# Delta rule of a hybrid decoder: one chain of small operations for two chunks, six places for chunks, four product tiles

## The chip, the cores and the metric

One core of a Trainium2 chip runs the whole program. The metric is the device time of one execution in microseconds (us). The engines are TensorE (PE; PEld is its weight load), VectorE (DVE), ScalarE (ACT), GpSimd (POOL) and SyncE (SP, which issues transfers). Differences of under some 0.5% are not told from no change here.

## What is computed

Two layers of a decoder, for 2048 prompt positions and 8 one-step samples. The first layer has two branches, a gated convolution and a gated delta rule with 4 heads of 128 channels; then memory attention; the second layer is a pooling mixer and memory attention again. The delta rule for one chunk of tokens (the kernel takes chunks of 128), shortened:

```python
q, k = l2_normalize(q), l2_normalize(k)
a_low = strict_lower(einsum('id,jd->ij', k * beta, k) * decay)
u, w = triangular_solve(I + a_low, [v * beta, k * beta * exp(gc)])
qk = lower(einsum('id,jd->ij', q, k) * decay)
# over the chunks, one after the other:
v_new = u - w @ S
o = (q * exp(gc)) @ S + qk @ v_new
S = S * exp(gc_last) + (k * exp(gc_last - gc)).T @ v_new
# then
o = rms_norm(o, dn_g) * silu(z)
```

The memory attention of a layer needs, for each head, products of the attention weights with the memory's keys (called G) and values (called VW). They depend on no token and can be computed at any time before the attention.

## The kernel before

**How the order comes about.** The program is one Python run that emits every instruction. A class `Flow` keeps a model of each engine's time and emits instructions at once: a main thread of large matmuls (`dense`), and between its groups of four matmuls the steps of side tasks (Python generators) whose data the model holds to be ready. So the order on each engine is fixed when the program is built, and depends on that model. `Flow.move` and `Flow.rows` (lines 191 and 201) also choose by the model whether ACT or DVE does a copy, and `ve` (line 210) whether DVE or POOL does a split. On the chip each engine takes its instructions in that order.

**The stages.** `phase1` (line 652) does the input projections of the first layer; it stores q, k, v after their short convolution to `d_qkv` and the gate z to `d_z` in device memory. `phase2` (line 1057) does the delta rule as side tasks, while the main thread is `Fill.run` (line 1011): 576 matmuls for G and VW, in 64 results of 128x512 that leave through tiles `gv`, of which there are two. Then `e2` (line 1479) does the output projection of the first layer, and the attention and the second layer follow.

**The delta rule.** 16 chunks of 128 tokens, in eight pairs.
- `prep(n)` (line 1103) loads k, q, v of a chunk, forms the decay matrix `dec`, the squared norms `ss` (ACT, with an accumulator), and from them the row factors `br`, all as columns of four heads: four small DVE operations, then `rsqrt` (line 410) with eleven more, then one more, each of 128x4. It leaves A, kd, qk, bv. A counter `slots` of eight places holds prep back: chunk n can start when chunk n-8 has left the scan. Six places lie in the pool `d2`, two in a pool `d3` that opens later.
- `inv16(t)` (line 1192) inverts 16x16 blocks of a pair on POOL; `levels(t)` (line 1215) builds the inverse of both chunks from them on TensorE (first matmuls: `ps_bg<-lo,A`). One `levels` runs at a time.
- `scan` (line 1295) goes through the chunks in order and carries the state S: matmuls `S,k` and `S,q`, then `x,A`, then `vn,kd` and `vn,qk`. Before `vn,kd` it takes one of three output tiles `o` (counter `ofree`).
- `onorms` (line 1342), two tasks, each for every second chunk: squares on ACT, 13 small DVE operations of 128x4 (two, then `rsqrt`), a scaling of o, a transpose (`ps_bg<-ident,o`), the product with z, a store to `d_b`. Only then the output tile is given back.

In the rows, L168 and L172 are the helpers for matmul and transpose, L186 is every ACT operation, L219, L225 and L232 to L238 are DVE or POOL operations, L313 is every transfer. So tiles tell the operations apart.

Of the kernel before, what the change touches and what calls it, by code (L numbers as in the profile page):

```python
# [436 lines left out]
def spread(F, C, pool, ppool, r, n, tag, dg=None):  # L437

    ncn = (n + 127) // 128
    if dg is None:  # L440
        dg = pool.tile([128, ncn * 128], F32, tag=tag + "dg", name="dg")
    for c in range(ncn):
        F.ts(dg[:, c * 128:(c + 1) * 128], C.ident, r[:, c:c + 1], ALU.mult)
    yield
    ps = ppool.tile([128, 512], F32, tag="bg", name="ps_bc")
    F.mm(ps[:, 0:n], C.ones, dg[:, 0:n])
    return ps
# [204 lines left out]
def phase1(F, C, I, D, st, P, R, mmp, bgp, loaders, mix, hp):  # L652
# [38 lines left out]
    with F.tile_pool(name="x1", bufs=1, side="right") as xp:  # L691
# [77 lines left out]
        def fin_z(b, t, n, ps):  # L769
# [3 lines left out]
            F.dma(D.z[b][:, o:o + n], z[:, 0:n])  # L773
# [148 lines left out]
    def conv4(b, t):  # L922
# [11 lines left out]
        F.dma(D.qkv[b][:, t * 512:(t + 1) * 512], z)  # L934
# [55 lines left out]
class Fill:  # L990
# [20 lines left out]
    def run(self):  # L1011
# [3 lines left out]
        for i, u in enumerate(self.units):  # L1015
# [41 lines left out]
def phase2(F, C, I, D, st, P, fill, hp, mmp, bgp, after):  # L1057
# [22 lines left out]
    def room(tag, n):  # L1080

        q, b = (dx, 2) if n % 8 in (4, 5) else (cq, SL - 2)
# [4 lines left out]
    SL = 8  # L1087
    slots, vfree = Res(SL), Res(3)
    nxt = [0]
    done = {"A": set(), "T": set(), "L": set(), "S": {-1}, "N": set(), "P": set(), "U": set()}  # L1090
# [4 lines left out]
    qkv = D.qkv.rearrange("(x h) p t -> x p h t", x=3)  # L1095
    zv = D.z.rearrange("h p t -> p h t")
# [6 lines left out]
    def prep(n):  # L1103
        yield lambda: nxt[0] == n and cq and (n < 4 or dx) and slots.n >= 2 - n % 2 and (n < SL or n // 2 - (SL+1)//2 in done["T"])
# [6 lines left out]
        tok = slice(128 * n, 128 * n + 128)  # L1111
# [3 lines left out]
        F.dma(X.k, qkv[1][:, :, tok])  # L1115
        F.dma(q, qkv[0][:, :, tok])
# [7 lines left out]
        ss = X.ss = cq.tile([128, 8], F32, tag="ss", name="ss", bufs=16)  # L1124
# [19 lines left out]
        for h in range(4):  # L1144
            j = cq.tile([128, 128], F32, tag="junk", name="junk", bufs=1)
            F.act(j, pq[:, h, :], AF.Square, accum=ss[:, h:h + 1])
        yield
# [40 lines left out]
        F.rows(X.bv, pv, br[:, 4:8])  # L1188
# [101 lines left out]
    def load_q(n):  # L1290
        q = big("q2", 2)
        F.dma(q, qkv[0][:, :, 128 * n:128 * n + 128])
        return q

    def scan():
# [5 lines left out]
        for n in range(16):  # L1301
# [6 lines left out]
            for h in range(4):  # L1308
                F.stt(x[:, h, :], pk[:, h, :], X.br[:, 8 + h:9 + h], X.bv[:, h, :], ALU.mult, ALU.add)
# [111 lines left out]
NG = 8  # L1421
# [1221 lines left out]
```

## Time and profile before

| | |
|---|---|
| median of 3 runs | 2901.84 us (2892.87 to 2902.51) |
| the profiled execution | 2902.86 us, its span 2901.1 us |
| busy: PE, DVE, ACT, POOL | 2730.5, 1968.4, 1032.0, 657.0 us |
| mean granted TensorE clock | 0.97 of full speed |

The stage of the delta rule lies at about 780 to 1210 us of the span; the first `Fill` matmuls come at about 820 us, and those of `e2` at about 1200 us. A column PEclk gives TensorE's granted clock as a share of its upper level. In a row of instructions, "[2.5 <-DVE S L225]" says that the engine was idle for 2.5 us before it, until that instruction of DVE had ended.

### The profile page before, as it was taken

The page shows a single profiled execution, that of the slowest core. Times are in us where ns is not written, and L with a number is a line of the kernel's source. Part 1 is how long each engine was busy: PE and PEld are TensorE (multiplying, and loading weights), DVE is VectorE, ACT ScalarE, POOL GpSimd, SP SyncE. Part 2 cuts the span into 40 slices and gives each one's busy share as a digit, 9 for nine tenths or more (in the row PEclk, how much of TensorE's full clock was granted, in tenths as well). Part 3 has the DMA queues.
Part 4 walks back from the last instruction along what each step waited for, and adds up shares of the span by engine and source line. Part 5 has one row for each costly group of instructions (what it writes and reads, how often), then busy time and mean ns, then how long its engine had stood idle before and what let it go on. Part 6 is the DMA issues. An engine that isn't in the chain of part 4 may idle for free.

```text
span 2901.1 us, 52440 instructions
## 1 busy us (share of the span) xinstructions
PE 2730.5 (94%) x20202; PEld 2498.5 (86%) x20202; DVE 1968.4 (68%) x4612; ACT 1032.0 (36%) x2448; POOL 657.0 (23%) x936
## 2 busy tenths in 40 slices
PE   7999999999998889799999999899999998999997
PEld 6878888888888778699898889899999997789987
DVE  6838999988667887776655556867755445765453
ACT  5632232233356455432321325443422122432321
POOL 3301112111054355122232320111011111221210
PEclk9999999999989899899999999999999999999998
DMA  7611122123455557565645434322545556422211
GB/s 240 213 48 41 46 75 65 46 77 113 129 148 160 154 165 230 172 228 183 211 149 169 144 117 140 116 70 74 173 134 165 181 165 206 136 78 68 70 59 52
DMA packets 269194, 377.85 MB, mean 130 GB/s; under 512 B 46096, under 2 KB 168208, under 8 KB 268944
## 3 DMA queue, kind: packets, MB, share of 16 engines
q1 hardware_dynamic: 211776, 264.77, 29.4%
q0 software_dynamic: 20864, 67.39, 7.5%
q10 hardware_dynamic: 36304, 42.34, 4.2%
q8 instruction: 159, 2.61, 0.4%
q14 instruction: 91, 0.75, 0.1%
HBM read 276.38 MB, written 96.40 MB: 128 GB/s over the span
## 4 chain that ended last, share of the span: by engine, by line
PE 34%; DMA 9%; DVE 6%; issue 2%; ACT 1%; POOL 1%; DVEq 0%; SPq 0%; POOLq 0%; ACTq 0%
PE ps_mm L168 32%; DMA a_big<-d_sp 2%; DVE a_big L225 1%; DMA a_big<-d_sq 1%; DMA a_big<-in_cache_v 1%; PE ps_pt L172 1%; DMA w_f<-d_x 1%; DVE rlo L225 1%; DVE w_d L219 1%; DMA rraw<-d_VW 1%; PE ps_row L168 1%; DVE rlo L219 1%; DVE ml L219 0%; DMA rraw<-d_G 0%; DMA a_big<-in_cache_k 0%
## 5 line engine op out<-in xcount | busy, mean ns | idle before, releaser
L219 POOL TENSOR_TENSOR rlo<-rraw,rhi 128x512 fp32r<-128x512 f32 x143 | 209.1, 1470 | 579.0 <-ACT rhi L186 495.5
L225 DVE SCALAR_TENSOR_TENSOR cacc<-glu,dww,cacc 128x1024 f32<-128x1024 f32 x240 | 325.6, 1369 | 5.9 <-ACT cacc L186 1.4
L219 POOL TENSOR_TENSOR w_sqb<-w_sqb,w_sqq 128x512 f32<-128x512 f32 (+1 forms) x101 | 137.1, 1357 | 660.9 <-ACT w_sqq L186 653.9
L168 PE MATMUL ps_mm<-xh,rhi 128*128 128x256 f32 (+1 forms) x1920 | 274.0, 285 | 5.3 <-DVE pool_sm L219 3.2
L168 PE MATMUL ps_mm<-xl,rhi 128*128 128x256 f32 (+1 forms) x1920 | 273.1, 284 | 0.0
L168 PE MATMUL ps_mm<-xh,rlo 128*128 128x256 f32 (+1 forms) x1920 | 272.7, 283 | 0.0
L168 PEld LDWEIGHTS ps_mm<-xh,rhi 128*128 128x128 f32 x1920 | 250.6, 192 | 8.6 <-issue 3.4
L168 PEld LDWEIGHTS ps_mm<-xl,rhi 128*128 128x128 f32 x1920 | 250.0, 192 | 2.6
L168 PEld LDWEIGHTS ps_mm<-xh,rlo 128*128 128x128 f32 x1920 | 248.2, 191 | 1.0
L168 PE MATMUL ps_mm<-hh,rhi 128*128 128x512 f32 (+2 forms) x1152 | 216.8, 329 | 20.2 <-ACT hh L186 15.8
L219 DVE TENSOR_TENSOR w_y<-ps_mm,w_y 128x256 f32<-128x256 f32 (+1 forms) x248 | 103.4, 420 | 165.6 <-PE ps_mm L168 161.2
L168 PE MATMUL ps_mm<-hh,rlo 128*128 128x512 f32 (+2 forms) x1152 | 214.6, 328 | 0.0
L168 PEld LDWEIGHTS ps_mm<-hh,rhi 128*128 128x128 f32 x1152 | 177.9, 191 | 42.0 <-ACT hh L186 16.2
L168 PE MATMUL ps_mm<-hl,rhi 128*128 128x512 f32 (+2 forms) x1152 | 211.7, 326 | 0.0
L225 DVE SCALAR_TENSOR_TENSOR a_big<-a_big 128x256 f32<-128x256 f32 x256 | 105.0, 448 | 144.5 <-DMA a_big<-d_sp 78.3
L186 ACT ACTIVATE rhi<-rraw 128x512 fp32r<-128x512 f32 x235 | 143.8, 628 | 164.0 <-DMA rraw<-d_G 41.5
L168 PEld LDWEIGHTS ps_mm<-hh,rlo 128*128 128x128 f32 x1152 | 175.9, 191 | 19.4 <-issue 2.2
L168 PEld LDWEIGHTS ps_mm<-hl,rhi 128*128 128x128 f32 x1152 | 175.4, 190 | 17.3
L168 PE MATMUL ps_mm<-mh,rhi 128*128 128x256 f32 (+1 forms) x1152 | 170.1, 288 | 11.8 <-ACT mh L186 11.7
L168 PE MATMUL ps_mm<-ml,rhi 128*128 128x256 f32 (+1 forms) x1152 | 170.5, 290 | 2.5 <-DVE ml L219 2.5
L168 PEld LDWEIGHTS ps_mm<-mh,rhi 128*128 128x128 f32 x1152 | 153.6, 195 | 14.5 <-ACT mh L186 12.8
L168 PE MATMUL ps_mm<-mh,rlo 128*128 128x256 f32 (+1 forms) x1152 | 165.6, 284 | 0.0
(425 smaller groups left out, 5344.5 us busy)
## 6 DMA issues: line engine op xcount, KB each, us to landing
w_f<-d_x SPq DMA_DIRECT2D x60, 512.0 KB
d_x<-w_y SPq DMA_DIRECT2D x44, 512.0 KB
w_y<-d_x SPq DMA_DIRECT2D x44, 512.0 KB
a_big<-in_cache_k POOLq DMA_DIRECT2D x64, 256.0 KB, 4.0
a_big<-in_cache_v POOLq DMA_DIRECT2D x64, 256.0 KB, 4.1
rraw<-in_w_in SPq DMA_DIRECT2D x56, 256.0 KB
d_qkv<-so ACTq DMA_DIRECT2D x48, 256.0 KB
rraw<-in_w_xk SPq DMA_DIRECT2D x32, 256.0 KB
```

The source lines that it names most:

```text
L168: self.nc.tensor.matmul(out, lhsT, rhs, start=start, stop=stop)
L172: self.nc.tensor.transpose(out, in_, ident)
L186: self.nc.scalar.activation(out=out, in_=in_, func=func, scale=scale, **kw)
L219: self._e(eng).tensor_tensor(out=out, in0=a, in1=b, op=op)
L225: self._e(eng).scalar_tensor_tensor(out=out, in0=a, scalar=s, in1=b, op0=op0, op1=op1, **kw)
```

## The change

- Two chunks of a pair share their small operations: `ss` is now one tile of 16 columns for a pair, `br` one of 32, and the even chunk's operations are done by the odd chunk together with its own, on 128x8. The even chunk waits for them. Likewise `onorms(t)` takes both chunks of a pair at once: it starts when both are out of the scan.
- Six places for chunks instead of eight, all in one pool; the pool `d3` is gone. The third to sixth chunk need not wait any more for the end of the projections.
- Four tiles `gv` instead of two. The loads for `Fill` begin one step later ("h3" instead of "h2").
- `d_qkv`, `d_z` and `d_b` have another layout: what prep, scan and onorms load is then one piece of 2 KB for each partition instead of four of 512 bytes; the stores of phase 1 have pieces of 512 bytes instead of 2 KB. For the columns at the tile borders there are 12 more stores of z, on ACT's queue.
- A counter `afree` bounds the chunks between loading v and storing their blocks to three. `spread` takes its PSUM pool when it needs it.

```diff
@@ fin_z, phase1
-            F.dma(D.z[b][:, o:o + n], z[:, 0:n])
...
+                if r == 0 and e - a >= 128:
+                    k = (e - a) // 128
+                    F.dma(D.z[c:c + k, :, b, :].rearrange("c p t -> p c t"), z[:, a - o:a - o + 128 * k].rearrange("p (c t) -> p c t", c=k))
...
@@ conv4, phase1
-        F.dma(D.qkv[b][:, t * 512:(t + 1) * 512], z)
+        F.dma(D.qkv[b // 4, 4 * t:4 * t + 4, :, b % 4, :].rearrange("c p t -> p c t"), z.rearrange("p (c t) -> p c t", c=4))
@@ Fill.run
-                    g = wp.tile([128, 512], F32, tag="gv", name="gv", bufs=2)
+                    g = wp.tile([128, 512], F32, tag="gv", name="gv", bufs=4)
@@ phase2
-        q, b = (dx, 2) if n % 8 in (4, 5) else (cq, SL - 2)
+        q, b = cq, SL
...
-    SL = 8
-    slots, vfree = Res(SL), Res(3)
+    SL = 6
+    slots, vfree, afree = Res(SL), Res(3), Res(3)
@@ prep
-        yield lambda: nxt[0] == n and cq and (n < 4 or dx) and slots.n >= 2 - n % 2 and (n < SL or n // 2 - (SL+1)//2 in done["T"])
+        yield lambda: nxt[0] == n and cq and slots.n >= 2 - n % 2 and (n < SL or n // 2 - (SL+1)//2 in done["T"])
...
+        ss = X.ss = cq.tile([128, 16], F32, tag="ss", name="ss", bufs=8) if n % 2 == 0 else hu[n - 1].ss
...
-        yield
+        done["K"].add(n)
+        yield lambda: n - c2 in done["K"]
...
-        br = X.br = cq.tile([128, 12], F32, tag="br", name="br", bufs=SL)
-        F.ts(br[:, 0:4], ss[:, 4:8], EPS, ALU.add)
-        F.recip(br[:, 4:8], br[:, 0:4])
-        F.tt(br[:, 4:8], br[:, 4:8], st.beta[:, :, n], ALU.mult)
-        F.stt(br[:, 8:12], br[:, 4:8], -1.0, gate["egc"][:, :, n], ALU.mult, ALU.mult)
+        if c2:
+            br = X.br = hu[n - 1].br = cq.tile([128, 32], F32, tag="br", name="br", bufs=SL // 2)
+            F.ts(br[:, 0:8], ss[:, 8:16], EPS, ALU.add)
+            F.recip(br[:, 8:16], br[:, 0:8])
...
+            done["B"].add(n // 2)
...
+        yield lambda: n // 2 in done["B"]
...
-        rsqrt(F, cq, br[:, 4:8], br[:, 0:4], 4, "pr")
-        F.tt(br[:, 4:8], br[:, 4:8], st.beta[:, :, n], ALU.mult)
-        yield
+        if c2:
+            rsqrt(F, cq, br[:, 24:32], br[:, 0:8], 8, "pr")
+            F.tt(hk(br[:, 24:32]), hk(br[:, 24:32]), st.beta[:, :, n - 1:n + 1], ALU.mult)
+            done["R"].add(n // 2)
+        yield lambda: n // 2 in done["R"]
@@ onorms
-    def onorms(i):
-        for n in range(i, 16, 2):
-            yield lambda: n in oq
+    def onorms(t):
+
+        yield lambda: {2 * t, 2 * t + 1} <= set(oq)
...
-            rsqrt(F, sq, f, os, 4, f"o{i}")
...
+        rsqrt(F, sq, f, os, 8, "o")
...
-    for i in range(2):
-        F.spawn(onorms(i), 1)
+    F.spawn(every(onorms, 0, 1, 8), 1)
@@ places
         sq = P("s2", 1, side="right")
+        yield lambda: "h3" in st.done
         F.spawn(fill.begin(), 2, front=True)
-        yield lambda: "h3" in st.done
         lp = P("l2", 1, side="right")
         yield lambda: st.done >= {"h4", "so"}
-        dx = P("d3", 1, side="right")
@@ build
-        D.qkv = dr.tile([12, 128, SEQ], F32, name="d_qkv")
-        D.z = dr.tile([4, 128, NT], F32, name="d_z")
+        D.qkv = dr.tile([3, 16, 128, 4, 128], F32, name="d_qkv")
+        D.z = dr.tile([16, 128, 4, 128], F32, name="d_z")
+        D.zs = dr.tile([128, 4, 8], F32, name="d_zs")
...
-        D.b = [dr.tile([4, 128, gn(g)], F32, name=f"d_b{g}") for g in range(NG)]
+        D.b = [dr.tile([128, 4, gn(g)], F32, name=f"d_b{g}") for g in range(NG)]
```

Since the order follows from the model, the change moves instructions on all engines. Over the whole program DVE has 4358 instructions before and 4184 now, ACT 2317 and 2260, POOL 941 and 933, TensorE the same number.

**VectorE, the small operations of `onorms`** (`ss`, `os`, `of`: sums and factors of the norm; `rt`, `ri`: scratch of `rsqrt`). Before, where the chain of one chunk ends and that of the next chunk begins, with a step of the scan (`x`) between:

```order
L225 SCALAR_TENSOR_TENSOR rt<-rt,os 128x4
L225 SCALAR_TENSOR_TENSOR of<-rt,of 128x4
L225 SCALAR_TENSOR_TENSOR x<-ps_bg,br,bv 128x128 x4
L234 TENSOR_SCALAR ss<-ss 128x4
L225 SCALAR_TENSOR_TENSOR os<-os,ss 128x4
L415 TENSOR_SCALAR ri<-os 128x4
L234 TENSOR_SCALAR of<-ri 128x4
L219 TENSOR_TENSOR rt<-of 128x4
```

Now, the beginning of the chain of the first pair:

```order
L234 TENSOR_SCALAR ss<-ss 128x8
L225 SCALAR_TENSOR_TENSOR os<-os,ss 128x8
L415 TENSOR_SCALAR ri<-os 128x8
L234 TENSOR_SCALAR of<-ri 128x8
L219 TENSOR_TENSOR rt<-of 128x8
L225 SCALAR_TENSOR_TENSOR rt<-rt,os 128x8
L225 SCALAR_TENSOR_TENSOR of<-rt,of 128x8
```

Sixteen such chains of 128x4 have become eight of 128x8, and likewise sixteen of `prep`.

**TensorE, the last pair's `levels`** (`lo,A` are its first matmuls, `b,UT` its next; `ps_mm` are `Fill`). Before:

```order
L168 MATMUL ps_bg<-x,A 128x128 x4
L168 MATMUL ps_bg<-lo,A 32x16 x32
L168 MATMUL ps_mm<-rhi 128x256 x2
L168 MATMUL ps_mm<-rlo,rhi 128x256 x2
L168 MATMUL ps_mm<-rhi,rlo 128x256 x2
```

Now:

```order
L168 MATMUL ps_mm<-rhi 128x512 x2
L168 MATMUL ps_mm<-rlo,rhi 128x512 x2
L168 MATMUL ps_mm<-rhi,rlo 128x512 x2
L168 MATMUL ps_bg<-lo,A 32x16 x32
L168 MATMUL ps_bg<-b_12716,UT 32x16 x32
```

Before, 48 of `Fill`'s 576 matmuls stand behind `lo,A` of the last pair; now 12 do.

**TensorE, the scan of chunk 13** (`vn,kd` and `vn,qk` end it; `ident,o` is an output transpose of `onorms`). Before:

```order
L168 MATMUL ps_mm<-rlo,rhi 128x256 x2
L168 MATMUL ps_mm<-rhi,rlo 128x256 x2
L168 MATMUL ps_bg<-vn,kd 128x128 x4
L168 MATMUL ps_bg<-vn,qk 128x128 x4
L168 MATMUL ps_bg<-b_12918,UT 32x16 x32
```

Now:

```order
L168 MATMUL ps_mm<-rhi,rlo 128x256 x2
L172 MATMUL ps_bg<-ident,o 128x128 x4
L168 MATMUL ps_bg<-vn,kd 128x128 x4
L168 MATMUL ps_bg<-vn,qk 128x128 x4
L168 MATMUL ps_mm<-rhi 128x512 x2
```

Now `vn,kd` stands right behind the output transpose of chunk 10, and 54 matmuls of `Fill` stand between the `x,A` of chunk 13 and it. The same holds for chunks 5, 7, 9 and 11, with 54 to 96 matmuls between.

## Rows read from the trace of the kernel before

**Rows 1.** The page, whole span: busy us (share) and instructions of each engine.

```profile
PE 2730.5 (94%) x20202; PEld 2498.5 (86%) x20202; DVE 1968.4 (68%) x4612; ACT 1032.0 (36%) x2448; POOL 657.0 (23%) x936
```

**Rows 2.** Stretches: length; busy PE, PEld, DVE, ACT, POOL; PEclk; DMA share; GB/s.

```profile
815.00:1165.00 350.00, 305.26 (x3800) 274.54 (x3798) 269.48 (x830) 195.74 (x661) 172.01 (x330) 0.91 0.60 173
1165.00:1200.00 35.00, 22.21 (x140) 20.13 (x141) 28.80 (x69) 18.42 (x48) 5.33 (x6) 0.76 0.58 174
1240.00:2900.00 1660.00, 1590.44 (x11535) 1492.14 (x11533) 982.06 (x2696) 513.63 (x1104) 329.26 (x445) 0.98 0.42 134
```

**Rows 3.** Waits of PE at 820 to 1200 us: total us, times, longest.

```profile
PE ps_bg L168 <- DVE S L225: 11.3, 5, 4.3
PE ps_bg L168 <- DVE lo L232: 9.7, 4, 4.3
PE ps_bg L168 <- DVE A L232: 8.9, 4, 3.3
```

**Rows 4.** Groups of DVE at 780 to 1440 us: busy us, mean ns, idle before.

```profile
L225 DVE SCALAR_TENSOR_TENSOR of<-rt,of 128x4 f32<-128x4 f32 x48 | 12.0, 249 | 1.7
...
L219 DVE TENSOR_TENSOR rt<-of 128x4 f32<-128x4 f32 x48 | 9.0, 187 | 1.6
...
L219 DVE TENSOR_TENSOR rt<-rstd 128x2 f32<-128x2 f32 x24 | 3.9, 161 | 0.8
...
L225 DVE SCALAR_TENSOR_TENSOR a_r<-rt,a_r 128x8 f32<-128x8 f32 x3 | 0.5, 168 | 0.1
```

**Rows 5.** The same view: two of the larger operations.

```profile
L219 DVE TENSOR_TENSOR rlo<-rraw,rhi 128x512 fp32r<-128x512 f32 x53 | 37.1, 716 | 8.3 <-ACT rhi L186 8.3
...
L238 DVE COPY ad<-A 32x128 f32<-32x128 f32 x29 | 7.3, 253 | 0.4
```

**Rows 6.** PE by time: start us, us, operation, [idle before it and its releaser].

```profile
977.07 2.08 PE L168 MATMUL ps_bg<-S,k 128*128 128x128 f32 x8 [4.27 <-DVE S L225]
...
1036.57 1.35 PE L172 MATMUL ps_bg<-ident,o 128*128 128x128 f32 x4 [3.61 <-ACT o L186]
...
1043.43 2.07 PE L168 MATMUL ps_bg<-S,k 128*128 128x128 f32 x8 [2.86 <-DVE S L225]
...
1168.07 0.65 PE L168 MATMUL ps_bg<-A 64*64 64x64 f32 x8 [3.33 <-DVE A L232]
```

**Rows 7.** DVE by time: stretched operations of the chains ahead of these waits.

```profile
973.43 2.73 DVE L225 SCALAR_TENSOR_TENSOR br<-rt,br 128x4 f32<-128x4 f32 x1
...
1033.91 1.39 DVE L225 SCALAR_TENSOR_TENSOR rt<-rt,os 128x4 f32<-128x4 f32 x1
...
1164.88 1.21 DVE L225 SCALAR_TENSOR_TENSOR of<-rt,of 128x4 f32<-128x4 f32 x1
```

**Rows 8.** PE by time: two waits behind a `gv` tile.

```profile
844.25 1.33 PE L168 MATMUL ps_bg<-ident,gc 128*128 128x128 f32 x8 [2.51 <-DVE A L232]
...
1162.44 0.73 PE L168 MATMUL ps_mm<-rhi 128*128 128x512 f32 x2 [1.22 <-DVE gv L238]
```

**Rows 9.** Three stretches of 20 us with these waits.

```profile
840.00:860.00 20.00, 17.22 (x106) 14.41 (x105) 14.77 (x33) 15.26 (x65) 7.07 (x6) 0.74 0.35 103
960.00:980.00 20.00, 12.63 (x79) 11.95 (x78) 17.96 (x51) 5.26 (x12) 13.50 (x29) 0.70 0.70 198
1160.00:1180.00 20.00, 15.45 (x120) 13.25 (x118) 15.04 (x47) 7.51 (x18) 2.67 (x4) 0.74 0.64 191
```

**Rows 10.** PE, PE, SP and PE by time: first and last `levels`, last pair's load and end.

```profile
826.09 1.05 PE L168 MATMUL ps_bg<-lo,A 32*32 32x16 f32 x64 [4.29 <-DVE lo L232]
...
1146.91 0.73 PE L168 MATMUL ps_bg<-lo,A 32*32 32x16 f32 x64
...
1049.82 0.43 SPq L313 DMA_DIRECT2D k<-d_qkv  x1
...
1192.97 1.17 PE L168 MATMUL ps_bg<-vn,qk 128*128 128x128 f32 x8
```

**Rows 11.** Groups of PE at 820 to 1440 us: `Fill` with 512 columns.

```profile
L168 PE MATMUL ps_mm<-rlo,rhi 128*128 128x512 f32 x64 | 22.2, 432 | 0.0
```

More of the change, by code (lines that the diff above doesn't have):

```diff
@@ L772, in fin_z @@
             F.act(z[:, 0:n], ps[:, 0:n], AF.Silu)
-            F.dma(D.z[b][:, o:o + n], z[:, 0:n])
+            a = o
+            while a < min(o + n, SEQ):
+                c, r = divmod(a, 128)
+                e = min(o + n, SEQ)
+                if r == 0 and e - a >= 128:
+                    k = (e - a) // 128
+                    F.dma(D.z[c:c + k, :, b, :].rearrange("c p t -> p c t"), z[:, a - o:a - o + 128 * k].rearrange("p (c t) -> p c t", c=k))
+                    a += 128 * k
+                else:
+                    k = min(128 - r, e - a)
+                    F.dma(D.z[c, :, b, r:r + k], z[:, a - o:a - o + k])
+                    a += k
+            if o + n > SEQ:
+                F.dma(D.zs[:, b, :], z[:, SEQ - o:NT - o])
         fin = {"z": fin_z}
@@ L1114, in prep @@
         q = small("q", NP, NP)
-        F.dma(X.k, qkv[1][:, :, tok])
-        F.dma(q, qkv[0][:, :, tok])
+        F.dma(X.k, D.qkv[1, n])
+        F.dma(q, D.qkv[0, n])
         yield
@@ L1145, in prep @@
             j = cq.tile([128, 128], F32, tag="junk", name="junk", bufs=1)
-            F.act(j, pq[:, h, :], AF.Square, accum=ss[:, h:h + 1])
-        yield
+            F.act(j, pq[:, h, :], AF.Square, accum=ss[:, 2 * h + c2:2 * h + c2 + 1])
+        yield lambda: n // 2 in done["B"]
+        br = X.br
         pa = ps4()
@@ L1151, in prep @@
         for h in range(4):
-            F.stt(X.A[:, h, :], pa[:, h, :], br[:, 4 + h:5 + h], dec[:, h, :], ALU.mult, ALU.mult)
-        yield vfree.ok
+            F.stt(X.A[:, h, :], pa[:, h, :], br[:, 8 + 2 * h + c2:9 + 2 * h + c2], dec[:, h, :], ALU.mult, ALU.mult)
+        yield lambda: vfree.ok() and afree.ok()
         vfree.take()
+        afree.take()
         v = small("v", 2 * NP, 3)
-        F.dma(v, qkv[2][:, :, tok])
+        F.dma(v, D.qkv[2, n])
         F.now()
@@ L1174, in prep @@
             F.dma(X.ia[i:i + 8], a16[:, h, :])
+        afree.give()
         done["A"].add(n)
@@ L1187, in prep @@
         X.bv = room("bv", n)
-        F.rows(X.bv, pv, br[:, 4:8])
+        F.rows(X.bv, pv, hk(br[:, 24:32])[:, :, c2])
         vfree.give()
@@ L1291, in load_q @@
         q = big("q2", 2)
-        F.dma(q, qkv[0][:, :, 128 * n:128 * n + 128])
+        F.dma(q, D.qkv[0, n])
         return q
@@ L1340, in scan @@
             F.dma(D.o_delta_p[h], S[h])
-    def onorms(i):
-        for n in range(i, 16, 2):
-            yield lambda: n in oq
-            o, ss = oq.pop(n)
-            z = sq.tile([128, 4, 128], F32, tag=f"z{i}", name="z", bufs=1)
-            F.dma(z, zv[:, :, 128 * n:128 * n + 128])
+    def onorms(t):
+        yield lambda: {2 * t, 2 * t + 1} <= set(oq)
+        os = sq.tile([128, 8], F32, tag="os", name="os", bufs=1)
+        o, z = [], []
+        for c in range(2):
+            oc, ss = oq.pop(2 * t + c)
+            o.append(oc)
+            z.append(sq.tile([128, 4, 128], F32, tag=f"z{c}", name="z", bufs=1))
+            F.dma(z[c], D.z[2 * t + c])
             F.now()
-            os = sq.tile([128, 4], F32, tag=f"os{i}", name="os", bufs=1)
+        for c in range(2):
             for h in range(4):
                 j = sq.tile([128, 128], F32, tag="junkq", name="junkq", bufs=1)
-                F.act(j, o[:, h, :], AF.Square, accum=os[:, h:h + 1])
+                F.act(j, o[c][:, h, :], AF.Square, accum=os[:, 2 * h + c:2 * h + c + 1])
             yield
-            F.ts(ss[:, 0:4], ss[:, 0:4], EPS, ALU.add, EPS * 128, ALU.mult)
-            F.stt(os, os, 1.0 / 128, ss[:, 0:4], ALU.mult, ALU.add)
-            f = sq.tile([128, 4], F32, tag=f"of{i}", name="of", bufs=1)
-            rsqrt(F, sq, f, os, 4, f"o{i}")
-            yield
-            F.rows(o, o, f)
+        F.ts(ss[:, 0:8], ss[:, 0:8], EPS, ALU.add, EPS * 128, ALU.mult)
+        F.stt(os, os, 1.0 / 128, ss[:, 0:8], ALU.mult, ALU.add)
+        f = sq.tile([128, 8], F32, tag="of", name="of", bufs=1)
+        rsqrt(F, sq, f, os, 8, "o")
+        yield
+        for c in range(2):
+            n = 2 * t + c
+            F.rows(o[c], o[c], f.rearrange("p (h c) -> p h c", c=2)[:, :, c])
             yield
@@ L1363, in onorms @@
             for h in range(4):
-                F.tr(pt[:, h, :], o[:, h, :], C.ident)
-            F.stt(z, pt, C.dng[:, 0:1], z, ALU.mult, ALU.mult)
-            F.dma(D.b[n // 2].rearrange("h p t -> p h t")[:, :, 128 * (n % 2):128 * (n % 2) + 128], z)
+                F.tr(pt[:, h, :], o[c][:, h, :], C.ident)
+            F.stt(z[c], pt, C.dng[:, 0:1], z[c], ALU.mult, ALU.mult)
+            F.dma(D.b[n // 2][:, :, 128 * (n % 2):128 * (n % 2) + 128], z[c])
             ofree.give()
@@ L1546, in prep @@
             b = W.t("f", [128, 4, n])
-            F.dma(b, D.b[g].rearrange("b p t -> p b t"))
+            F.dma(b, D.b[g])
             tb = F.cur
@@ L2217, in sample_mix @@
     yield lambda: "z" in st.done
-    F.dma(zs, D.z.rearrange("h p t -> p h t")[:, :, SEQ:NT])
+    F.dma(zs, D.zs)
     F.tt(kd, o, o, ALU.mult)
```

23 lines of the change are left out of this document (11 added, 12 removed).

## The prediction, written before the changed kernel was run

> **What bounds the kernel now.** I read the page first: TensorE is busy for 94% of the span [rows 1]. Then I asked for the busy times stage by stage, and the reader should see where the missing 6% lie. Behind the delta rule, from 1240 to 2900 us, the clock is 0.98, and the change touches none of the work there [rows 2]. In the stage of the delta rule TensorE is idle for 350 - 305.3 = 44.7 us up to 1165 us and for 35 - 22.2 = 12.8 us in the next 35 us, its mean clock is 0.91 and 0.76, and DVE is busy for 269.5 of 350 us, 77% [rows 2]. So this stage has 57.5 us of idle time, and time at the lower clock besides.
>
> Next, whom TensorE waits for there. The three longest entries are all DVE: the state S, `lo` and A, 29.9 us together [rows 3]. None of these is a long operation. The timeline shows what stands ahead of them on DVE: chains of small operations. The S update that ends a wait of 4.27 us stands right behind the whole `rsqrt` of a prep, of which one operation alone took 2.73 us [rows 6, 7]. A wait of 3.33 us for A ends at 1168.07 us, behind a chain of `onorms` with one operation of 1.21 us [rows 6, 7]. The waits of 3.61 and 2.86 us at 1036.57 and 1043.43 us fall in and behind two such chains, one after the other, the first with an operation of 1.39 us [rows 6, 7]. Two other waits, of 2.51 and 1.22 us, come from the two `gv` tiles: DVE was to write one whose store had not ended, and what TensorE waited for was that copy or stood behind it [rows 8].
>
> **The change, part by part.** The profiled execution took 2902.86 us; the sum is made against that. It is 1.0 us over the median of the runs.
>
> *Small operations.* Before, each chunk has 4 + 11 + 1 in prep and 2 + 11 in `onorms`: 29, for 16 chunks 464. Now 232. One costs between 187 and 249 ns by the groups of 48 [rows 4]. Eight columns have no row in prep, but an operation of 128x8 elsewhere took 168 ns where one of 128x2 took 161 ns [rows 4], so I take width as free. That removes between 43 and 58 us of DVE time; I take 50 (215 ns). But DVE has only 174 instructions fewer in all, since the planner gives it 58 others. Those are copies and splits, between 253 and 716 ns each [rows 5]: 15 to 42 us, and I take 0.45 us each, in the middle, as the order shows both kinds: 26 us. DVE loses some 24 us net (1 to 43).
>
> What of it lies on TensorE's path? First, the four waits behind chains, 4.27 + 3.61 + 2.86 + 3.33 = 14.1 us [rows 6]. Half of the chains go, so I take 7.0 us (0 to 14.1). Second, the other waits for S, `lo` and A: 29.9 less 4.27, 2.86, 3.33 and 2.51 is 16.9 us [rows 3, 6, 8]. DVE has 80.5 us free up to 1165 us and would have 104.5, 30% more [rows 2], so I take 30% of them, 5.1 us (0 to 16.9).
>
> *Four product tiles.* The two waits of 2.51 and 1.22 us go: 3.7 us [rows 8]; at worst nothing, if the next store is as late.
>
> *Clock.* Three stretches with these waits have 0.74, 0.70 and 0.74 [rows 9]. With two levels, 2.4 and 1.2 GHz, a mean of 0.70 is 60% of 20 us, 12.0 us, at the lower one, and 0.74 is 10.4 us: 32.8 us, in which TensorE did half the work, so at most 16.4 us are lost. In each the lower clock goes with a wait that I shorten by half or remove; I take 8.2 us (0 to 16.4).
>
> *The end of the stage.* 36 matmuls of `Fill` that now cover the last pair's `levels` are put ahead of it. One with 512 columns took 22.2 / 64 = 0.347 us [rows 11]. Where TensorE is the bound ahead of `lo,A`, that is 12.5 us more; where it waits there anyway, nothing. I take half, 6.0 us more, since TensorE is mostly busy but not always.
>
> *Edits at nothing.* The even chunk waits for the odd one of its pair, and the scan of an odd chunk waits for the norm of an earlier pair: matmuls of `Fill` stand between, 54 to 96 of them; if that cover is gone, the next rival is what happens. Behind the waiting `vn,kd` stand the next chunk's S, and behind that its slot. The 12 more z stores on ACT's queue, and the stores in smaller pieces, fall before 815 us; nobody reads z before the first norm. The loads of k, q, v and z have a quarter of the pieces, on SP's queue, but TensorE's waits for them are not among the long ones [rows 3], so they give nothing. `Fill`'s first loads come later, but it starts only when the projections end.
>
> Sum: 7.0 + 5.1 + 3.7 + 8.2 - 6.0 = 18.0 us. The forecast is 2902.9 - 18.0 = 2884.9, rounded 2885 us. With all terms at their best 51.1 us go (2852 us), at their worst 12.5 us are added (2915 us).
>
> **The rivals.** *The waits only change their names* (no difference). S, x and v follow one another in the scan; `levels` is a chain of eight steps, each matmul and copy. If TensorE waits for these chains as such, then shorter DVE chains beside them give little, and DVE's own saving is 1 us at the low end. For it: DVE has gaps, 80.5 us, so it is not full [rows 2]. Against it: the four waits end just behind small operations [rows 6, 7]. Time: only the `gv` term stands, and the end of the stage takes it back: 2902.9 - 3.7 + 6.0 = 2905 at most, 2892 with half of the first terms; I say 2899.
>
> The page "Perfetto Trace Analysis" of the Trainium skill ("Identifying the Most-Contended Engine") says to optimise the engine with the highest occupancy first; by the whole span that is TensorE, whose instructions stay the same, and by that alone the time would stay 2902.9 us. The same section warns that matmul busy share is no good measure of how near TensorE is to its limit, and the next one has the regimes taken apart; the stage's rows agree with that, with 57.5 us idle.
>
> *Six places make the round too long* (slower). With eight places four pairs are under way, with six only three: a pair's load waits until the pair three before it has left the scan. The last pair took from its load at 1049.82 us to the end of its last matmuls at 1194.1 us, 144 us [rows 10]. `levels` followed one another every (1146.91 - 826.09) / 7 = 45.8 us [rows 10]. Three rounds of that are 137 us, and this is the point: a pair that takes longer from load to scan's end sets the pace. At 144 us the pace is 48.1 us, for the five pairs that must wait 11 us more; with the new wait of the scan for the norm, 54 matmuls of 0.347 us or 18.7 us at most, it is 163 us, a pace of 54.3, and 42 us more. The middle is 27 us; less 7 us of the gains (`gv` and half of the chains), 2902.9 + 20 = 2923 us, between 2907 and 2938. For it: 144 is over 137. Against it: part of the 144 us is waiting for the one `levels` task, which a later start would not lengthen, and shorter chains shorten the round itself.
>
> *All of it goes* (much faster): all terms near their best, since nearly every wait on DVE lies behind a chain that goes; 2862 us, between 2852 and 2872.
>
> **How the numbers follow.** The forecast has a chance of 0.45 (2872 to 2897), no difference 0.27, six places 0.18, all of it 0.10. Faster by over 0.5% means under 2888.4 us, 14.5 us below (no less can be told from no change): three quarters of the forecast (0.34), all of the large gain (0.10), a little of no difference (0.02): 0.46. Slower by over 0.5%, over 2917.4, are two thirds of six places (0.12) and a little of no difference (0.02): 0.14. The rest, 0.40, is the same. The range from 2858 to 2916 leaves out half of the large gain (0.05) and the upper part of six places (0.13), and contains the bounds of the sum but for the best 6 us.
>
> **What would show it.** In the changed profile the stage from 815 to 1200 us should be some 18 us shorter, with DVE near 70% busy, fewer than 45 us idle on TensorE and a clock of 0.92 or more; no wait for a `gv` store; waits for S, `lo` and A of under 22 us together. Step by step: small operations of 128x8 at 250 ns or less, or the first term is wrong; the stretch from the last `lo,A` to the first matmul of `e2` shows the end's term. The six places are at fault if the k loads of late pairs come right behind the scan's end of the third pair before, and TensorE is idle ahead of `lo,A` with the chain behind it all the time at work. The forecast is wrong if the stage keeps its length with DVE lighter, or if the time goes in the stages behind, which I hold equal.

## The result, and the profile after

| | before | after |
|---|---|---|
| median, same chip | 2902.18 us (12 runs) | 2886.24 us (12 runs) |
| ratio | | 0.9947 [0.9935, 0.9960] |
| profiled execution, its span | 2902.86, 2901.1 us | 2889.38, 2887.7 us |

The change takes 15.9 us off by the medians, 0.53% by the ratio: just over the bound of 0.5%, which lies inside the interval. The forecast was 2885 us.

The page of the changed kernel answers to [rows 1]. TensorE is as full as before; DVE has lost 174 instructions and 20.0 us.

```profile
PE 2721.9 (94%) x20202; PEld 2494.4 (86%) x20202; DVE 1948.4 (67%) x4438; ACT 1012.6 (35%) x2388; POOL 647.4 (22%) x928
```

The stretches of [rows 2] in the changed kernel, and a fourth one, from 820 us to its first matmul of `e2` (same columns):

```profile
815.00:1165.00 350.00, 311.64 (x3933) 283.90 (x3932) 271.22 (x737) 190.99 (x637) 163.41 (x320) 0.93 0.62 184
1165.00:1200.00 35.00, 20.26 (x113) 18.39 (x112) 24.29 (x54) 16.73 (x39) 2.29 (x2) 0.68 0.42 132
1240.00:2900.00 1660.00, 1572.93 (x11383) 1476.18 (x11382) 964.62 (x2660) 505.01 (x1090) 328.83 (x448) 0.98 0.41 131
...
820.00:1180.90 360.90, 311.53 (x3913) 283.23 (x3912) 278.04 (x746) 194.61 (x646) 163.41 (x320) 0.91 0.62 184
```

The same stretch of the kernel before, whose first matmul of `e2` comes at 1200.4 us:

```profile
820.00:1200.40 380.40, 322.87 (x3900) 290.07 (x3899) 293.76 (x884) 211.64 (x702) 174.92 (x330) 0.89 0.61 175
```

The fourth line is the one to read, since a window with fixed ends takes in more of the next stage when this one gets shorter. The stage lost 19.5 us: 11.3 us of TensorE's busy time for nearly the same matmuls (3900 and 3913, with the clock at 0.91 for 0.89), and 8.2 us of its idle time (57.5 before, 49.4 now). At the end 15.9 us of it are left by the medians, 13.5 us between the two profiled executions.

What TensorE waits for at 820 to 1200 us, which answers to [rows 3] (total us, times, longest):

```profile
PE ps_mean L168 <- DVE w_sqa L246: 11.0, 1, 11.0
PE ps_bg L168 <- DVE lo L232: 5.4, 3, 2.8
PE ps_bg L172 <- DVE o L219: 5.0, 2, 4.0
...
PE ps_bg L168 <- DVE S L225: 2.6, 2, 2.0
...
PE ps_bg L168 <- DVE A L232: 2.3, 1, 2.3
```

S, `lo` and A cost 10.3 us together instead of 29.9. But the longest wait is new, one of 11.0 us for `w_sqa`, in the norm of `e2`.

DVE's groups, answering to [rows 4, 5] (busy us, mean ns):

```profile
L238 DVE COPY ad<-A 32x128 f32<-32x128 f32 x47 | 12.3, 261 | 0.8
L219 DVE TENSOR_TENSOR rt<-of 128x8 f32<-128x8 f32 x24 | 5.1, 213 | 0.8
L225 DVE SCALAR_TENSOR_TENSOR of<-rt,of 128x8 f32<-128x8 f32 x24 | 5.1, 210 | 0.8
```

Over all groups of the two chains the 232 operations of 128x8 took 53.3 us, 230 ns each, where the 464 of 128x4 took 109.3 us, 235 ns each: 128x8 costs no more, and there are half as many. The Trainium skill says why few wide operations are to be had for less ("VectorE: DVE Perf Modes", "The TRN2 errata"): an operation from SBUF pays a fixed extra cost per instruction. The rows agree, with 230 ns for twice the width against 235 ns. The copies `ad<-A` are those that the planner gave back, 47 now for 29.

TensorE by time, answering to [rows 10]: first `levels`, chunk 9 in the scan, the last two `levels`, then the end of the stage.

```profile
825.14 0.72 PE L168 MATMUL ps_bg<-lo,A 32*32 32x16 f32 x64 [2.77 <-DVE lo L232]
...
1014.35 1.06 PE L168 MATMUL ps_bg<-x,A 128*128 128x128 f32 x8
...
1050.43 0.60 PE L172 MATMUL ps_bg<-ident,o 128*128 128x128 f32 x4
1050.87 1.06 PE L168 MATMUL ps_bg<-vn,kd 128*128 128x128 f32 x8
1051.76 1.06 PE L168 MATMUL ps_bg<-vn,qk 128*128 128x128 f32 x8
...
1074.61 0.72 PE L168 MATMUL ps_bg<-lo,A 32*32 32x16 f32 x64 [0.80 <-DVE lo L232]
...
1129.74 0.73 PE L168 MATMUL ps_bg<-lo,A 32*32 32x16 f32 x64
...
1166.99 1.13 PE L168 MATMUL ps_bg<-vn,qk 128*128 128x128 f32 x8
1179.14 1.22 PE L168 MATMUL ps_mean<-w_sqa,ones 128*128 128x256 f32 x2 [11.01 <-DVE w_sqa L246]
```

And SP's queue: the first load of k for the last pair, and one for `e2`.

```profile
1053.84 0.61 SPq L313 DMA_DIRECT2D k<-d_qkv  x1
...
1170.85 0.43 SPq L313 DMA_DIRECT2D w_d<-d_c  x1
```

Two things are to be seen. Chunk 9 has its `x,A` at 1014 us and its `vn,kd` only at 1051, right behind an output transpose: it waited 36 us for an output tile. The last pair's first load follows 1 us behind chunk 9's end. The last `levels` comes 55.1 us behind the one before it, and that one 55.2 us behind its own (1019.4 us), where the first five intervals averaged (1019.4 - 825.1) / 5 = 38.9 us; before, the seven went from 31 to 57 us. This reads as if the scan were held by the norm, and the last pairs by the scan; e10 tests it.

### The profile page after: what moved, and what is told of

It reads as the page before. It is cut to its first block, busy times and chain, and to the rows that moved or that the text cites. A ratio compares the mean times of both kernels' runs of the same rounds, so it can differ in the third digit from the quotient of the medians.

```text
span 2887.7 us, 52194 instructions
## 1 busy us (share of the span) xinstructions
PE 2721.9 (94%) x20202; PEld 2494.4 (86%) x20202; DVE 1948.4 (67%) x4438; ACT 1012.6 (35%) x2388; POOL 647.4 (22%) x928
## 4 chain that ended last, share of the span: by engine, by line
PE 51%; DVE 22%; DMA 11%; issue 4%; ACT 3%; POOL 1%; SPq 1%; DVEq 0%; ACTq 0%; POOLq 0%
PE ps_mm L168 44%; DVE cacc L225 7%; PE ps_bg L168 4%; DVE qacc L225 3%; DMA a_big<-d_sq 2%; DMA rraw<-d_VW 1%; DVE a_big L225 1%; DMA w_f<-d_x 1%; DMA a_big<-d_sp 1%; DVE rlo L219 1%; PE ps_pt L172 1%; PE ps_row L168 1%; DMA rraw<-d_G 1%; PE ps_bg L172 1%; POOL w_sqb L219 1%
## 5 line engine op out<-in xcount | busy, mean ns | idle before, releaser
L219 POOL TENSOR_TENSOR rlo<-rraw,rhi 128x512 fp32r<-128x512 f32 x132 | 197.3, 1505 | 552.8 <-ACT rhi L186 487.0
L186 ACT ACTIVATE rhi<-rraw 128x512 fp32r<-128x512 f32 x224 | 137.4, 630 | 176.6 <-DMA rraw<-d_G 43.0
L168 PEld LDWEIGHTS ps_mm<-mh,rhi 128*128 128x128 f32 x1152 | 153.7, 196 | 11.3 <-ACT mh L186 9.8
```

Source lines behind the costliest of these rows:

```text
L168: self.nc.tensor.matmul(out, lhsT, rhs, start=start, stop=stop)
L186: self.nc.scalar.activation(out=out, in_=in_, func=func, scale=scale, **kw)
L219: self._e(eng).tensor_tensor(out=out, in0=a, in1=b, op=op)
```

## The experiments

All ratios are to the kernel before, on the chip of the same job; "changed" is 0.9947, and 0.9944 when it was run again. The stretch from 820 us to the first matmul of `e2`, from a line as above for each kernel (us; idle is length less busy). The last two columns are counted along TensorE's timeline: the us of the span at which the last `vn,qk` of the scan ends, and at which the 384th matmul of `e2` with `xh` or `xl` starts.

| kernel | ratio [95%] | stretch | PE idle | DVE busy | clock | scan's end | 384th of `e2` |
|---|---|---|---|---|---|---|---|
| before | 1 | 380.4 | 57.5 | 293.8 | 0.89 | 1194.1 | 1285.2 |
| changed | 0.9947 [0.9935, 0.9960] | 360.9 | 49.4 | 278.0 | 0.91 | 1168.1 | 1265.9 |
| e1 short chains | 0.9958 [0.9942, 0.9973] | 369.3 | 51.6 | 256.6 | 0.92 | 1184.9 | 1274.7 |
| e2 changed, 232 more | 1.0083 [1.0066, 1.0100] | 398.3 | 78.8 | 313.5 | 0.87 | 1204.1 | 1301.8 |
| e3 another order | 1.0024 [1.0014, 1.0035] | 382.7 | 62.3 | 295.3 | 0.90 | 1199.7 | 1290.3 |
| e4 changed, two `gv` | 0.9957 [0.9942, 0.9972] | 354.7 | 51.5 | 260.0 | 0.93 | 1175.1 | 1268.2 |
| e5 e4's with eight places | 1.0040 [1.0025, 1.0056] | 381.7 | 64.3 | 270.6 | 0.89 | 1199.7 | 1295.7 |
| e6 changed, eight places | 1.0008 [0.9994, 1.0021] | 373.9 | 61.1 | 270.3 | 0.90 | 1169.1 | 1282.0 |
| e7 six places alone | 1.0014 [1.0003, 1.0025] | 382.2 | 64.7 | 286.8 | 0.91 | 1201.5 | 1291.5 |
| e8 changed, early load | 0.9993 [0.9981, 1.0004] | 361.6 | 53.9 | 282.1 | 0.92 | 1167.3 | 1273.9 |
| e9 changed, again | 0.9944 [0.9930, 0.9958] | 360.9 | 49.6 | 277.6 | 0.91 | 1168.2 | 1264.9 |
| e10 changed, four `o` | 0.9904 [0.9888, 0.9920] | 334.2 | 33.8 | 269.3 | 0.96 | 1148.4 | 1248.0 |
| e11 changed, norm by chunk | 0.9982 [0.9970, 0.9993] | 360.8 | 52.5 | 299.0 | 0.94 | 1156.4 | 1273.9 |
| e12 e10's, 232 more | 1.0039 [1.0024, 1.0053] | 369.2 | 58.1 | 304.8 | 0.91 | 1181.4 | 1285.6 |

### e1: fewer small operations, the order kept

The kernel before, with one Newton round instead of three. The lines cut here still charge the planner's model, so the order stays:

```diff
-    for _ in range(3):
+    for i in range(3):
+        if i and tag in ("pr", "o0", "o1"):
+            ...
+            continue
```

> The kernel before, with the order of all engines held, but each rsqrt of prep and onorms does one Newton round instead of three (the last two rounds are left out, so its factors are rougher): 192 small DVE operations of 128x4 fewer, some 40 us of DVE time. Theory (small DVE operations ahead of what TensorE waits for): the stage of the delta rule gets 8 to 20 us shorter, the time falls to 2882 to 2894 us. Rival (the order that the planner makes decides, not the work): less than 4 us, 2898 to 2902 us.

Measured 12.2 us less. The theory holds: with every other instruction in its place, fewer small operations give most of what the change gave. Each chain is also shorter here, 5 operations where `rsqrt` had 11, which the change does not do; e1 does not tell the two apart. It is little for 37 us of DVE time (293.8 to 256.6 us). Part of the rest shows in DVE's own waits at 815 to 1200 us:

```profile
DVE gv L232 <- ACT gv L186: 13.7, 5, 5.3
DVE gv L232 <- DMA d_G<-gv: 7.1, 2, 5.6
DVE gv L238 <- DMA d_G<-gv: 5.2, 1, 5.2
DVE gv L238 <- DMA d_VW<-gv: 4.8, 2, 3.9
```

The stores add up to 17.1 us here and to 8.5 us in the kernel before, the waits for ACT's copy to 13.7 and 2.0 us. A lighter DVE comes sooner to a `gv` copy whose tile is not free.

### e2: the removed number put back

```diff
     rsqrt, tags "pr" and "o":
+        for _ in range(16 if tag == "pr" else 13):
+            F.nc.vector.tensor_tensor(out=e, in0=x, in1=x, op=ALU.mult)
```

> The changed kernel, same order, with as many small operations of 128x8 as the change removed (232) put back behind each rsqrt, on a scratch tile. Theory (small DVE operations): 8 to 20 us longer, 2894 to 2906 us, by waits of TensorE for S, lo, A behind them. Rival (order): within 4 us of 2886 us.

Measured 1.0083 against 0.9947: some 40 us more than changed, twice the upper end of the theory, so its range is missed. The operations themselves took (groups of DVE):

```profile
L424 DVE TENSOR_TENSOR re<-br 128x8 f32<-128x8 f32 x128 | 22.8, 178 | 4.1
L424 DVE TENSOR_TENSOR re<-os 128x8 f32<-128x8 f32 x104 | 21.1, 203 | 3.3
```

43.9 us: nearly all of their time reached the end. At that point there were two explanations: the norm's chain lies on the scan's path (the hold above), or DVE as a whole bounds the stage. e12 tells them apart.

### e3 and e4: another order; two `gv` tiles

e3 changes a limit of the planner's model in the kernel before, so that some hundred rows of TensorE stand elsewhere; e4 is the changed kernel with two `gv` tiles.

```diff
-        F.LIM = (1500.0, 3800.0, 1000000000.0)
+        F.LIM = (1500.0, 3600.0, 1000000000.0)
```
```diff
-                    g = wp.tile([128, 512], F32, tag="gv", name="gv", bufs=4)
+                    g = wp.tile([128, 512], F32, tag="gv", name="gv", bufs=2)
```

> The kernel before, with one limit of the planner in this stage at 3600 instead of 3800 ns: the same operations, in an order that differs at some hundred rows of TensorE. It shows what a reordering by itself is worth. If orders are worth little: within 5 us of 2902 us. If the order is a lottery as large as the change: 8 us or more, either way.

> The changed kernel with two gv tiles instead of four. Theory of the prediction: the term of 3.7 us comes back, with waits of DVE and ACT for stores of gv: 2888 to 2893 us. Rival one (four tiles carry most of the change): 2896 us or more. Rival two (they carry nothing): 2884 to 2888 us.

e3: 7.0 us more, between the two values named. An order alone is worth that much here, so a gain of 3 or 4 us has no cause of its own until more than one order shows it. e4: 0.10% more than changed, some 3 us, inside both intervals. The waits did come back, on ACT and on DVE. ACT's waits for the `gv` stores in e4 at 815 to 1200 us, of which the changed kernel has none of its own:

```profile
ACT gv L186 <- DMA d_G<-gv: 12.8, 6, 7.4
ACT gv L186 <- DMA d_VW<-gv: 9.7, 5, 2.9
```

ACT is busy for 193.2 of 354.7 us in the stage, so 22.5 us of waits there can cost little. But DVE waits for these stores too, 18.0 us in four entries; why that costs no more is not shown. e4's order differs as well.

### e5 to e7: the parts one by one

e7 is the kernel before with `SL = 6` and one pool; e6 the changed kernel with the two pools and eight places; e5 that, with two `gv` tiles as well.

```diff
-    SL = 6
+    SL = 8
...
-        q, b = cq, SL
+        q, b = (dx, 2) if n % 8 in (4, 5) else (cq, SL - 2)
...
```

> The changed kernel with eight places in two pools and two gv tiles, as before the change; the shared small operations, the layout in device memory and the later Fill loads stay. Theory (the shared small operations make the gain): 8 to 15 us less than before, a ratio of 0.995 to 0.9975; the stage's first e2 matmul at 1180 to 1192 us of the span, waits of TensorE for S, lo and A together under 18 us. Rival (the gain came from the gv tiles and a lucky order at six places): within 4 us of before, first e2 matmul at 1196 us or later.

> The changed kernel with eight places in two pools as before the change, four gv tiles. Theory (six places cost something at the end of the stage, as the last two levels lie 55 us apart where the first seven lie 42 us apart, but are no pace for the whole stage): 3 to 10 us less than the changed kernel, a ratio to before of 0.991 to 0.9937, last lo,A before 1125 us. Rival (the round is not the bound; places are free): 0.9937 to 0.996, the same as the changed kernel within the 7 us that another order alone was worth. Second rival (the longer hold of early places fills the chip's queues and DVE sooner): over 0.996.

> The kernel before with six places in one pool, nothing else changed: small operations of 128x4 for each chunk, two gv tiles. Theory (three pairs under way pace the stage only where a pair takes longer than three levels): 3 to 12 us more than before, a ratio of 1.001 to 1.004, k loads of the late pairs right behind the scan's end of the third pair before. Rival of the prediction (the round of 144 us sets the pace for five pairs): 11 us or more, over 1.004. Rival (places are free): within 3 us of before, 0.999 to 1.001.

e5 is a miss and the most telling one: 11.6 us slower than before, with 23 us less DVE time in the stretch (270.6 for 293.8 us). Sharing the small operations is no gain by itself here. e6 falls where its second rival put it: eight places cost 0.6% more than six; the reason that the rival gave, fuller queues, is not shown. e7 is near the low edge of its theory, 4.1 us more, and its interval takes in the rival of free places. So neither part gains alone, and together they give 16 us: the parts don't add. Each is shown in the one order that the planner made for it, and the changed kernel was not run on the chip of e5 to e8.

The waits of TensorE in e5 at 820 to 1200 us show what took the saving:

```profile
PE ps_bg L168 <- DVE S L225: 12.2, 6, 4.2
PE ps_bg L172 <- DVE o L219: 11.1, 2, 9.0
PE ps_mm L168 <- ACT gv L186: 9.9, 3, 6.4
```

The longest wait for `o` (9.0 us, at 1196 us) is for the output of a shared norm, and the last chunk's `vn,kd` stands behind it. The hold of the scan is there too: chunk 9 took 45.1 us from `S,k` to `vn,kd`, and the scan ended later than before. In e6 the scan ends where the changed kernel's does (1169.1 and 1168.1 us), so its loss lies behind the scan, much of it in one wait:

```profile
1192.30 1.11 PE L168 MATMUL ps_ss<-ones,w_sqa 128*128 128x64 f32 x4 [13.64 <-POOL w_sqa L219]
```

What feeds it stands behind this in DVE's order: DVE stood 6.85 us for a weight of the output projection:

```profile
1184.77 0.43 DVE L238 CAST rhi<-rraw 128x512 fp32r<-128x512 f32 x1 [6.85 <-DMA rraw<-in_w_out_e]
```

### e8: an early load against the new wait

```diff
+            if g == 0:
+                load(0)
+                load(1)
...
```

> The changed kernel with the loads of e2's first two groups of gated columns both issued at the start of e2's norms, so that the second group's mean doesn't wait for a load issued as late as 1171 us. Theory (the one wait of 11.0 us of TensorE for w_sqa at 1179 us is the path there, with the scan's last steps queued behind it): 5 to 11 us less than the changed kernel, a ratio to before of 0.991 to 0.993, no wait for w_sqa over 3 us and the first e2 matmul before 1176 us. Rival (what stands behind, the last pair's levels, was late anyway): within 3 us of the changed kernel, the wait then named x, b or Uc.

A miss on the worse side: 0.9993, where the changed kernel had 0.9947 and 0.9944. The wait of 11.0 us fell to 7.0, and others stand behind it (TensorE by time):

```profile
1174.80 1.19 PE L168 MATMUL ps_mean<-w_sqa,ones 128*128 128x256 f32 x2 [7.01 <-DVE w_sqa L246]
1180.76 1.11 PE L168 MATMUL ps_ss<-ones,w_sqa 128*128 128x64 f32 x4 [4.78 <-POOL w_sqa L219]
...
1215.01 1.19 PE L168 MATMUL ps_bc<-w_sqq,ones 128*128 128x256 f32 x2 [4.83 <-DVE w_sqq L232]
```

The load was the last of several things that `e2` waits for, so the wait changed its name. The scan's end and the first matmul of `e2` are within 1 us of the changed kernel's; the 384th comes 8.0 us later (1273.9, 1265.9 us).

### e9 to e11: the hold of the scan

e9 is the changed kernel itself. e10 has one more output tile, e11 the old `onorms` with its two tasks; all else as changed.

```diff
-    b3free, oq, ofree = Res(1), {}, Res(3)
+    b3free, oq, ofree = Res(1), {}, Res(4)
-            o = big("o", 3)
+            o = big("o", 4)
```
```diff
...
-    F.spawn(every(onorms, 0, 1, 8), 1)
+    for i in range(2):
+        F.spawn(onorms(i), 1)
```

> The changed kernel itself, unchanged, on the chip of the next two kernels, so that differences of a few us to it are taken on one chip. Theory: a ratio to before of 0.9935 to 0.996, as found first; rival (the ratio depends on the chip by some tenths of a per cent): 0.996 to 0.999. The second would put the early load's 0.9993 within noise of the changed kernel.

> The changed kernel with four output tiles o instead of three; the room is there since two places went. In the changed kernel the scan's step vn,kd of each odd chunk came right behind an output transpose of the pair before, up to 40 us after its x,A (chunk 7: S,k at 1011 us, vn,qk at 1052 us). With four tiles the order has at most 12 Fill matmuls between where 54 to 96 stood. Theory (the shared norm holds the scan, and through its places the next preps and levels): last lo,A at 1105 to 1122 us instead of 1130, first e2 matmul before 1177 us, 3 to 12 us less than the changed kernel. Rival (TensorE is busy with Fill meanwhile, and the wait is in the order alone): the Fill matmuls only change places, within 4 us of the changed kernel.

> The changed kernel with the norms by chunk again, as before the change (two tasks, 13 operations of 128x4 for each chunk, 104 small operations more on DVE), all else as changed. Theory A (the number of small operations on DVE is what counts): 5 to 20 us more than the changed kernel, as 192 operations fewer gave 12 us before the change and 232 more cost 40 us after it. Theory B (sharing the norm costs what its fewer operations give, since the even chunk's output tile is held until the odd one is out): 0 to 12 us less than the changed kernel, the scan's end before 1160 us, no vn,kd more than 15 us behind its x,A. Sharing in prep alone would then be the part that gains.

(The chunk named there as 7 is chunk 9, counted from 0.) e9 repeats the first result. e10 beats both kernels: 2875.71 us, 0.9904, some 12 us less than e9 on the same chip, at the upper edge of its theory and more than the 7.0 us of e3's order. Its TensorE by time, chunk 9, the last `levels` and a wait in `e2`:

```profile
1023.69 1.06 PE L168 MATMUL ps_bg<-x,A 128*128 128x128 f32 x8
...
1026.44 1.05 PE L168 MATMUL ps_bg<-vn,kd 128*128 128x128 f32 x8
...
1100.35 0.73 PE L168 MATMUL ps_bg<-lo,A 32*32 32x16 f32 x64
...
1179.25 1.19 PE L168 MATMUL ps_mean<-w_sqa,ones 128*128 128x256 f32 x2 [8.54 <-DVE w_sqa L246]
```

and SP's load of the last pair:

```profile
1028.12 0.96 SPq L313 DMA_DIRECT2D k<-d_qkv  x1
```

`vn,kd` now follows its `x,A` after 3 us; the load comes 26 us earlier, the last `levels` 29 us, the first matmul of `e2` 26.7 us. TensorE's idle time in the stage falls from 49.4 to 33.8 us and the clock rises to 0.96. Not all of it reaches the end: with the wait of 8.54 us in `e2`, which e9 does not have there, the 384th matmul of `e2` comes 16.9 us earlier than in e9, and the medians differ by 12 us. With three output tiles the odd chunks 5, 7, 9, 11 and 13 took 20.5, 27.6, 39.6, 37.7 and 16.4 us from `S,k` to `vn,kd`; with four none took over 8 us. (In the kernel before only chunks 7 and 9 took over 13 us, 29.8 and 15.9.) The Trainium skill ("Perfetto Trace Analysis", "Optimization Strategy") has a line near this: the same gap repeating on the engine that should be saturated can mean that there isn't room for the next tile. Here too a tile was missing, but the trace differs in one point: the 16 to 40 us were no gap of TensorE, which had `Fill` to do, but a distance between two steps of the scan.

e11 takes the hold away in another way and pays for it with 104 more small operations: by the time it is theory A, 0.38% or 11 us more than e9. By the stage it is theory B: the scan ends at 1156.4 us, no `vn,kd` comes more than 10.3 us behind its `x,A`, and the stage is as short as the changed kernel's (360.8 and 360.9 us). The loss comes behind it, in waits of TensorE at 1180 to 1480 us:

```profile
PE ps_ss L168 <- POOL w_sqa L219: 15.8, 3, 9.9
PE ps_mean L168 <- DVE w_sqa L246: 6.3, 5, 3.7
PE ps_bc L168 <- DVE w_sqq L232: 5.8, 3, 3.9
```

In the changed kernel they have hardly any in the same window (`ps_bc` none):

```profile
PE ps_ss L168 <- POOL w_sqa L219: 2.9, 5, 0.9
...
PE ps_mean L168 <- DVE w_sqa L246: 0.4, 1, 0.4
```

So e11's DVE has the norms of the stage and those of `e2` one behind the other; I read that from the names of the waits and did not test it.

### e12: the same load without the hold

e10 with the 232 extra operations of e2.

> The kernel with four output tiles, and behind each shared rsqrt of prep and of the norms as many operations of 128x8 on a scratch tile that nobody reads as the change had taken away: 232 more small DVE operations, the order of all else as with four tiles. With three output tiles the same 232 cost some 40 us. Theory (with three tiles the chain of the norm lies on the scan's path, since the scan stands still until an output tile is back; with four it lies beside it): 8 to 25 us more than with four tiles, a ratio to before of 0.993 to 0.999. Rival (DVE's time is the bound of the stage, whatever the scan waits for): 35 us or more, over 1.002.

Measured 1.0039 against 0.9904, 39 us more, as much as e2. The operations themselves (groups of DVE):

```profile
L424 DVE TENSOR_TENSOR re<-br 128x8 f32<-128x8 f32 x128 | 23.0, 179 | 4.1
...
L424 DVE TENSOR_TENSOR re<-os 128x8 f32<-128x8 f32 x104 | 17.3, 167 | 3.3
```

The theory falls and the rival holds by the time: the scan isn't held any more (odd chunks take at most 8.9 us from `S,k` to `vn,kd`), and small operations on DVE still cost nearly their whole 40.3 us. DVE is not full even so, 304.8 of 369.2 us: the price comes by the chains that stand behind them. TensorE's waits at 820 to 1200 us show where it lands:

```profile
PE ps_bg L168 <- DVE x L225: 10.2, 3, 4.7
PE ps_bg L168 <- DVE S L225: 8.6, 4, 3.9
PE ps_bg L168 <- DVE Uc L219: 7.0, 2, 4.2
```

and its stretch to the first matmul of `e2`:

```profile
820.00:1189.20 369.20, 311.10 (x3888) 281.17 (x3889) 304.76 (x915) 196.54 (x652) 160.68 (x321) 0.91 0.59 176
```

against that of e10:

```profile
820.00:1154.20 334.20, 300.42 (x3892) 269.17 (x3891) 269.26 (x717) 195.54 (x651) 162.25 (x321) 0.96 0.66 195
```

35.0 us more in the stage: 24.3 us of idle time on TensorE and 10.7 us of busy time for nearly the same matmuls, with the clock down from 0.96 to 0.91. So the price of these operations has two parts, the waits and the clock that falls with them.

## Why the prediction was right, step by step

The time (2885 for 2886.2 us) and the main mechanism were right. The terms were not all, and that the sum came within 1.3 us is in part luck: a gain larger than taken and a wait that the sum didn't have offset each other.

- **Small operations.** 128x8 at 230 ns on average where 215 was taken, and 56 us of small operations removed where 50 were; DVE lost 20.0 us net by the page where 24 was taken. Right. Four groups in prep were over the 250 ns of the mark (262 to 381 ns); single operations were stretched there as before.
- **Waits for S, `lo` and A.** 12.1 us were taken, a wait for `o` among them; the three entries fell by 19.6 us. Mis-sized, in the direction of more. But the gain wasn't kept: total idle time in the stage fell by 8.2 us only, because the wait for `w_sqa` came instead.
- **Product tiles.** The `gv` stores no longer hold anyone. Taken 3.7 us; e4 has some 3 us, not told from nothing.
- **Clock.** 8.2 us taken; TensorE's busy time in the stage fell by 11.3 us. Right in kind and roughly in size. The mark of 0.92 from 815 to 1200 us was missed: 0.90, for 0.89 before.
- **End of the stage.** 6.0 us more were taken, since `Fill` matmuls no longer stand behind the last `levels`. From the last `lo,A` to the first matmul of `e2` it was 53.5 us before and is 51.1 us now, with 36 matmuls of `Fill` fewer in it. So it did not shrink by their time, as the term assumed, and the wait of 11.0 us now stands in it; no run measures the 6.0 us alone. What the term left out is that the last `levels` itself came late, for the reason in the next point.
- **Edits at nothing.** This is the step that failed. The prediction saw that the scan of an odd chunk now waits for the norm of an earlier pair and let the `Fill` matmuls hide it. They did fill TensorE's time there, but they are the cover that the end of the stage then lacks (12 of them stand behind the last `lo,A`, 84 in e10), and the last pair's loads hang on chunk 9. e10 takes the wait away and gains 12 us, three quarters of what the whole change gave. Its price stood in the rival of six places alone, as 18.7 us for 54 matmuls; chunk 9, with 96 of them, waited 36 us.
- **Six places.** The rival of 2923 us fell: e7 costs 4.1 us, and e6 shows eight places to be slower in this kernel. But a part of it did come, in its form with the wait for the norm (163 us, a pace of 54.3 us). The first load of each of the last four pairs stands within 5 us of the end of the third pair before. The rounds of the pairs with chunks 9 and 11 are 1052.8 - 899.2 = 153.6 and 1100.0 - 946.7 = 153.4 us, over three `levels` of 43.5 us, and the last two `levels` come at 55 us. In e10, without the hold, these rounds are 136.5 and 138.4 us. The last pair's round is 1168.1 - 1053.8 = 114 us instead of 144.
- **"Waits only change their names."** It fell as a whole (e1), but it is what happened to e8, and to e5.
- **Marks.** DVE was to be near 70% in the stage: it is 77% as before (271.2 of 350, 278.0 of 360.9 us), since stage and work shrank together; that mark was a poor one. Under 45 us idle in the two fixed stretches: 38.4 + 14.7 = 53.1 us, wrong, because of the end.

What stays open: why eight places are worse than six once the operations are shared. In e6 the scan ends as early as with six, and the loss is behind it, with a wait of 13.6 us as one part; whether that belongs to the places or to the order, which alone was worth 7 us in e3, no run tells. Nor does one tell why so much of what the scan gains is lost where `e2` begins (e6, e10, e11).

## What to carry over

Where a planner keeps the main engine full, an added wait in a side chain doesn't show as idle time: look at what the waiting step releases (here a place, through it the last pair) and at which work was spent as its cover, and try one more tile for the chain. When two steps share small operations, the first holds its buffers until the second is there, so count the buffers again; here three output tiles were one too few. Judge a part of such a change in the kernel where it is to stand: neither shared operations nor six places gained alone. And follow a gain past the end of its stage: here the next stage's first waits took part of it back.

## What the runs showed that I had not expected

- Small operations on a DVE that is busy for 77 to 81% of the stage cost their full time when added (232 for some 40 us, twice), but only a third came back when 37 us were taken from the kernel before (12.2 us).
- A lighter DVE raised TensorE's granted clock in the stage (0.89 to 0.92 in e1, with the order kept), a heavier one lowered it (0.96 to 0.91 in e12): about a third of the cost in e12 is the busy time that this adds.
- The stretched small operations go with GpSimd. At 780 to 1240 us of the kernel before, 27 of the 464 small operations of the chains took over 350 ns, and each of them ended 17 to 30 ns behind the end of an operation of POOL, as only 50 of the other 437 did. The one of 2.73 us [rows 7] ended at 976.16 us, POOL's split at 976.14 us. In the changed kernel 18 of 232 took over 350 ns, and 16 of them ended so. No run takes POOL's work away: this is a reading of the rows and not a test.
